# A hybrid decoder layer on one core: x is loaded a second time in eight pieces between weight loads, and the pooling states pass through a staging tile

## The chip, the core and the metric

The kernel runs on one core of one Trainium2 chip. The metric is the device time of one execution in microseconds; the median of 3 runs of the kernel before is 1449.35 (1449.04 to 1449.45).

The engines are called as in the profile: PE (matrix multiply), DVE (vector), ACT (scalar), POOL (GpSimd) and SP (it only issues DMAs). SP's DMAs run on one hardware queue, POOL's on a software queue; both are served by the core's 16 DMA engines.

## The reference, cut to what matters

One layer for 256 prompt tokens and 8 sequences of 8 sample tokens (320 columns in all), model width 2048:

```python
h = rms_norm(x, norm_mix_pre)
proj = h @ w_in                     # q, k, v, g for 4 retention heads, u for 4 pooling groups
...
ret_out = silu(g) * group_norm(retention(q, k, v, S0))
xp = concatenate([buf, u], axis=1)              # buf: the last 15 rows of u, the pooling state
pooled = (windowed sums of xp over 2/4/8/16) / count - u
new_buf = xp[:, -15:, :]                        # an output
pool_out = (pooled per group @ w_pool) * pool_scale
mix = concatenate([ret_out, pool_out]) @ w_out
x = x + rms_norm(mix, norm_mix_post)            # x is needed a second time here
hf = rms_norm(x, norm_ffn_pre)
x = x + rms_norm((silu(hf @ w_gate) * (hf @ w_up)) @ w_down, norm_ffn_post)
```

Outputs are x for all tokens, the new retention states, and `new_buf` for prompt and samples.

## The kernel before, in words

Everything is held transposed, channels on the 128 partitions and the 320 tokens along the row. All matrix products run in three passes of split fp32 (`mm3`, L152 to L156): high weights by high x (L154), high weights by low x (L155), low weights by high x (L156).

**Weights.** The list `queue` holds all weight pieces of 512 KB (128 x 2 x 512) in order of use: `in` (10 groups of 8), `wo` (4 groups of 8, the output projection), then `gu` and `dn` of the feed-forward part. `prepare` (L168) does three things for a piece: SP issues its load into one of four `raw` buffers (L177); ACT casts it to `hi` (L146); DVE computes `lo` = raw - hi (L149). A raw buffer is free again when its `lo` is computed. `hi` and `lo` have four buffers each, free when PE has used the piece. A piece is split two pieces ahead of its use, from wo0 on three. An entry of `queue` can carry a function that runs just before its load; the first eight `in` pieces use it to load `x` for the first time (`xt`).

`project` (L194) runs one group: for each of its 8 pieces (here called chunks) 24 matmuls into four PSUM accumulators. Between chunks it runs side work from a list `stages`, spread evenly by `spread` (L184).

**The stretch around the change.** The order of use is: four heads (qk and vg each), then u1 and u0 (the inputs of pooling groups 3, 2 and 1, 0), then wo0 to wo3. The stages of one group run inside the next: those of the last head inside u1, those of pooling groups 3 and 2 (`pool_group(1, ...)`) inside u0, those of groups 1 and 0 inside wo0. wo0 uses the heads' chunks first and then those of groups 3, 2, 1, 0.

A pooling group has a tile `ue` (in a buffer that a retention state `s_raw` held before), with 15 zero columns, the 256 prompt columns and 8 segments of 15 state columns and 8 new ones. `pool_group` fills it: POOL loads the states (L526), DVE writes u (L527, L528). The stage `windows` stores the new states (L538, L540), loads the group's `w_pool` (`wp`, L542), and adds the windows on DVE (`uw`). `means` gives `pl`, split into `pc` (ACT cast, DVE rest; helper L332, L333), and splits `wp` into `wph` and `wpl`. `mapped` multiplies them on PE (`pp`) and splits the result into `mi_h` and `mi_l` (L336, L337), which wo0's later chunks read.

**The second x.** Behind wo0's code, `x_t` takes over the buffer of `xw_l`, which PE reads until u0 ends, and SP loads all of x into it with one DMA (L616). It is read behind wo3, when the norm of `mix` is there.

Within each engine the order of instructions is set by a scheduler of the framework, from the order and the dependences of the code; each engine then works through its list strictly in order.

Of the kernel before, what the change touches and what calls it, by code (L numbers as in the profile page):

```python
# [18 lines left out]
F32 = mybir.dt.float32  # L19
F32R = mybir.dt.float32r  # L20
# [4 lines left out]
P = 128  # L25
D = 2048
KT = D // P
T = 320
TP = 256
TS = 64  # L30
NB = 8
NS = 8
# [5 lines left out]
PB = 15  # L38
# [60 lines left out]
def layer_kernel(ctx, tc, x, vec, trig, con, mask, pool_in, s_ret, w_in, w_pool, w_out, w_gu, w_dn,  # L99
                 y, o_rp, o_pp, o_rs, o_ps, decay):  # L100
    nc = tc.nc
# [32 lines left out]
    def keep_warm(n, name):  # L134

        ps = aux(f"warm_{name}")
        for i in range(n):
            nc.tensor.matmul(ps[:, :P], ones, ones, start=True, stop=True)
# [20 lines left out]
    queue, raws, parts = [], {}, {}  # L159
    at = dict(load=0, split=0, use=0, ahead=AHEAD[0])  # L160
# [6 lines left out]
    def prepare(between=None):  # L167
        while at["split"] < min(at["use"] + at["ahead"], len(queue)):  # L168
            while at["load"] < min(at["split"] + RAW, len(queue)):
                n = at["load"]  # L170
                src, name, before, _ = queue[n]
                raws[n] = wp.tile([P, 2, 512], F32, tag="raw", name=f"raw_{name}", bufs=RAW)
                step = 1 if n == 0 else 2
                for k in range(0, 2, step):
                    if before:
                        before(k, step)
                    nc.sync.dma_start(out=raws[n][:, k : k + step], in_=src[:, k : k + step])  # L177
                at["load"] += 1
            n = at["split"]
            if queue[n][3]:  # L180
                queue[n][3]()
            parts[n] = halves(raws.pop(n), queue[n][1], 1 if n == 0 else 2, between)
            at["split"] += 1
# [10 lines left out]
    def project(xh, xl, kts, name, stages=(), feed=None, late=0):  # L194

        accs = [psm.tile([P, 512], F32, tag="acc", name=f"acc_{name}_{b}") for b in range(4)]
        n = len(kts) // 2
        steps = spread(stages, n)
        for c in range(n):
            hi, lo = next_weights(feed and (lambda: feed(c)))  # L200
            pairs = [(b, k) for b in range(4) for k in range(2)]
            if c < late:
                pairs.sort(key=lambda bk: bk[1])
            for b, k in pairs:
                bs = slice(b * P, b * P + P)
                kt = kts[2 * c + k]
                mm3(accs[b][:, :T], (hi[:, k, bs], lo[:, k, bs]), (xh[:, kt, :], xl[:, kt, :]),
                    start=c == 0 and k == 0, stop=c == n - 1 and k == 1)
            next(steps)
        return [a[:, :T] for a in accs]  # L210
# [9 lines left out]
    def add_eps(out, acc, sq, width):  # L220

        nc.vector.scalar_tensor_tensor(out, acc, EPS * width / P, sq, op0=ALU.add, op1=ALU.add)

    def slot(i, dtype, name, n=KT):
        return slots.tile([P, n, T], dtype, tag=f"s{i}", name=name)

    xw_h = slot(0, F32R, "xw_h")
    xw_l = slot(1, F32R, "xw_l")
# [4 lines left out]
    order = list(range(2 * H)) + [14, 15, 12, 13, 10, 11, 8, 9]  # L233

    with ExitStack() as ret_ctx:
# [43 lines left out]
        for g in [*range(2 * H), 2 * H + 1, 2 * H]:  # L279
            for c in range(8):  # L280
                queue.append((w_in[g, c], f"in{g}_{c}", (lambda k, step, c=c: x_load(c, k, step)) if g == 0 else None,
                              (lambda c=c: x_split(c)) if g == 0 else None))
        queue += [(w_out[og, order[2 * c] // 2], f"wo{og}_{c}", None, None) for og in range(4) for c in range(8)]
        g0 = 0
        for ph, ng in enumerate(PHASES):
            queue += [(w_gu[g, c], f"gu{g}_{c}", None, None) for g in range(g0, g0 + ng) for c in hf_order]
# [1 line left out]
            g0 += ng  # L288

        r_x = rp.tile([P, T], F32, name="r_x")  # L290
        cs = rp.tile([P, T], F32, name="cs")
        sn = rp.tile([P, T], F32, name="sn")

# [223 lines left out]
        def pool_group(gp, accs):  # L517

            stages = []
            for g_ in (1, 0):  # L520
                g = 2 * gp + g_
                ue = ext(s_raw(f"ue{g}").rearrange("p a e -> p (a e)"))
                us = ue[:, :, PB + TP :].rearrange("p e (b s) -> p e b s", s=SEG)
                nc.gpsimd.memset(ue[:, :, :PB], 0.0)
                for e in range(2):
                    nc.gpsimd.dma_start(out=us[:, e, :, :PB], in_=pool_in[:, 2 * g + e])  # L526
                    nc.vector.tensor_tensor(ue[:, e, PB : PB + TP], accs[2 * g_ + e][:, :TP], r_x[:, :TP], op=ALU.mult)  # L527
                    nc.vector.tensor_tensor(us[:, e, :, PB:], accs[2 * g_ + e][:, TP:].rearrange("p (j b) -> p b j", b=NB),  # L528
                                            r_x[:, TP:].rearrange("p (j b) -> p b j", b=NB), op=ALU.mult)
                stages += pool_stages(g, ue, us)  # L530
            return stages

        def pool_stages(g, ue, us):
            w = WINDOWS[g]
            st = {}

            def windows():
                nc.gpsimd.dma_start(out=o_pp[:, 2 * g : 2 * g + 2], in_=ue[:, :, TP : PB + TP])  # L538
                for e in range(2):
                    nc.gpsimd.dma_start(out=o_ps[:, 2 * g + e], in_=us[:, e, :, NS:])  # L540
                raw = rp.tile([P, 2, TP], F32, tag="st", name=f"wp{g}").rearrange("p a e -> p (a e)")
                nc.gpsimd.dma_start(out=raw, in_=w_pool[g])  # L542
                cur, step, lo_ = ue, 1, 0
                while step < w:
                    shape, tag = ([P, 2, 2, T], "cat_k") if step in (1, 4) else ([P, 2, 2, DK], "kv")
                    flat = rp.tile(shape, F32R, tag=tag, name=f"uw{g}_{step}").bitcast(F32)
                    nx = ext(flat.rearrange("p a s e -> p (a s e)"))
                    lo_ += step
                    nc.vector.tensor_tensor(nx[:, :, lo_:], cur[:, :, lo_:], cur[:, :, lo_ - step : EXT - step], op=ALU.add)
                    cur, step = nx, 2 * step  # L550
                st.update(cur=cur, raw=raw)

            def means():
                cur = st["cur"]
                pl = t640(f"pl{g}")
                nc.vector.scalar_tensor_tensor(pl[:, :, :TP], cur[:, :, PB : PB + TP], 1.0 / w, ue[:, :, PB : PB + TP],
                                               op0=ALU.mult, op1=ALU.subtract)
                for e in range(2):
                    fix = rp.tile([P, PB], F32, tag="fix", name=f"fix{g}_{e}", bufs=2)
                    nc.vector.tensor_tensor(fix, cur[:, e, PB : 2 * PB], cst("rcnt", PB * g, PB), op=ALU.mult)  # L560
                    nc.vector.tensor_tensor(pl[:, e, :PB], fix, ue[:, e, PB : 2 * PB], op=ALU.subtract)
                    nc.vector.scalar_tensor_tensor(
                        pl[:, e, TP:].rearrange("p (j b) -> p b j", b=NB),
                        cur[:, e, PB + TP :].rearrange("p (b s) -> p b s", s=SEG)[:, :, PB:], 1.0 / w,
                        us[:, e, :, PB:], op0=ALU.mult, op1=ALU.subtract)
                pc = rp.tile([P, 2, 2, T], F32R, tag="cat_q", name=f"pc{g}")
                split2(pc[:, 0], pc[:, 1], pl)
                wh = rp.tile([P, 2, TP], F32R, tag="sd_h", name=f"wph{g}").rearrange("p a e -> p (a e)")
                wl = rp.tile([P, 2, TP], F32R, tag="sd_l", name=f"wpl{g}").rearrange("p a e -> p (a e)")
                split2(wh, wl, st["raw"])  # L570
                st.update(pc=pc, wh=wh, wl=wl)

            def mapped():
                pc, wh, wl = st["pc"], st["wh"], st["wl"]
                for e in range(2):
                    ps = aux(f"pp{g}_{e}")
                    for t in range(2):
                        ws = slice(t * DK + e * P, t * DK + e * P + P)
                        mm3(ps[:, :T], (wh[:, ws], wl[:, ws]), (pc[:, 0, t], pc[:, 1, t]), start=t == 0, stop=t == 1)
                    kt = 2 * H + 2 * g + e  # L580
                    split2_scaled(mi_h[:, kt], mi_l[:, kt], ps[:, :T], col("pool_s", 2 * g + e))

            return [windows, means, mapped]
# [4 lines left out]
        def tables():  # L588
            nc.gpsimd.dma_start(out=con_t, in_=con)

        keep_warm(8, "first")
        stages = [idle, idle, tables, lambda: s_load(0), lambda: s_load(1), x_norm]
        for h in range(H):
# [6 lines left out]
                accs = kept  # L600
            stages = head(h, accs, lambda st: project(xw_h, xw_l, range(KT), f"vg{h}", st))
        for gp in (1, 0):
            accs = project(xw_h, xw_l, range(KT), f"u{gp}", stages)
            stages = pool_group(gp, accs)
        at["ahead"] = AHEAD[1]
        accs = project(mi_h, mi_l, order, "wo0", stages + [idle])
# [5 lines left out]
        return fp.tile([P, T], F32, tag="t320", name=name, bufs=6)  # L612

    mix = slot(0, F32, "mix")
    x_t = slot(1, F32, "x_t")
    nc.sync.dma_start(out=x_t, in_=x)  # L616

    def add_square(acc, src, i, name):

# [216 lines left out]
```

## Time and profile before

| | us |
|---|---|
| median of 3 runs | 1449.35 |
| the profiled execution | 1456.14 |
| its span, first to last instruction | 1454.3 |
| PE busy | 1416.4 |
| DVE busy | 755.3 |
| ACT busy | 574.3 |
| POOL busy | 102.3 |

Mean granted clock of PE over the span: 0.988 of full speed. The DMA engines move 233.83 MB, 161 GB/s on average. Busy shares are averages over stages with different limits; where time is lost must be read from the windows and from what each engine waits for.

### The profile page before, as it was taken

To read this page: it belongs to the slowest core of one execution; us is meant where nothing else is said; L and a number is where in the kernel's file an instruction comes from. 1 tells how busy PE (TensorE), PEld (TensorE's weight loads), DVE (VectorE), ACT (ScalarE), POOL (GpSimd) and SP (SyncE) were. 2 spreads that over 40 slices of the span, in tenths; PEclk is the share of its full clock that TensorE was granted. 3 is DMA by queue.
4 is the path that set the end of the run, shared out by engine and by line. 5 is a ranking of instruction groups with operands and counts; after the bars stand their busy time and mean duration, and the time that the engine had idled before them with its cause. 6 is when DMAs were issued, how large, how long until landed. Compare 5 with 4: busy or idle time off the path is not lost.

```text
span 1454.3 us, 22899 instructions
## 1 busy us (share of the span) xinstructions
PE 1416.4 (97%) x9576; PEld 1396.8 (96%) x9576; DVE 755.3 (52%) x981; ACT 574.3 (39%) x732; POOL 102.3 (7%) x153
## 2 busy tenths in 40 slices
PE   8999999999799889999999999999999999999995
PEld 8999999999799889999999999999999999999995
DVE  7657575767443694454334444444454534444455
ACT  6445454543244453333333333223333323333352
POOL 1020202042000340000000000000000000000000
PEclk9999999999899999999999999999999999999998
DMA  9484848488744345445444444444444444444442
GB/s 322 141 258 145 263 142 260 144 233 137 189 146 152 99 131 167 147 145 157 148 148 154 148 145 148 156 147 154 150 145 156 149 146 155 149 145 147 158 131 73
DMA packets 66824, 233.83 MB, mean 161 GB/s; under 512 B 8224, under 2 KB 10208, under 8 KB 66592
## 3 DMA queue, kind: packets, MB, share of 16 engines
q1 hardware_dynamic: 56304, 204.20, 45.4%
q0 software_dynamic: 10416, 28.17, 6.6%
q8 instruction: 75, 1.23, 0.4%
q14 instruction: 29, 0.24, 0.0%
HBM read 216.28 MB, written 16.05 MB: 160 GB/s over the span
## 4 chain that ended last, share of the span: by engine, by line
PE 89%; DMA 3%; DVE 3%; issue 2%; ACT 1%; POOL 1%; SPq 0%; DVEq 0%; ACTq 0%; POOLq 0%
PE acc_gu L156 14%; PE acc_gu L155 14%; PE acc_gu L154 14%; PE acc_dn L156 7%; PE acc_dn L155 7%; PE acc_dn L154 7%; PE acc_qk L154 3%; PE acc_qk L155 3%; PE acc_qk L156 3%; PE acc_vg L155 3%; PE acc_vg L154 3%; PE acc_vg L156 3%; PE acc_wo L156 2%; PE acc_wo L155 2%; PE acc_wo L154 2%
## 5 line engine op out<-in xcount | busy, mean ns | idle before, releaser
L155 PE MATMUL acc_gu<-hf_l,hi_gu 128*128 128x320 f32 x1408 | 437.5, 311 | 5.2 <-DVE hf_l L673 5.1
L154 PE MATMUL acc_gu<-hf_h,hi_gu 128*128 128x320 f32 x1408 | 436.9, 311 | 0.9 <-ACT hf_h L700 0.9
L156 PE MATMUL acc_gu<-hf_h,lo_gu 128*128 128x320 f32 x1408 | 433.8, 310 | 1.6 <-DVE lo_gu L149 1.6
L149 DVE TENSOR_TENSOR lo_gu<-raw_gu,hi_gu 128x1024 fp32r<-128x1024 f32 x176 | 217.9, 1238 | 272.6 <-ACT hi_gu L146 272.6
L146 ACT CAST hi_gu<-raw_gu 128x1024 fp32r<-128x1024 f32 x176 | 184.6, 1049 | 347.6 <-PE acc_gu L155 315.8
L155 PEld LDWEIGHTS acc_gu<-hf_l,hi_gu 128*128 128x128 f32 x1408 | 265.8, 189 | 7.2 <-DVE hf_l L673 7.1
L154 PEld LDWEIGHTS acc_gu<-hf_h,hi_gu 128*128 128x128 f32 x1408 | 265.8, 189 | 1.5 <-ACT hf_h L700 1.1
L156 PEld LDWEIGHTS acc_gu<-hf_h,lo_gu 128*128 128x128 f32 x1408 | 265.1, 189 | 1.9 <-DVE lo_gu L149 1.9
L154 PE MATMUL acc_dn<-a_h,hi_dn 128*128 128x320 f32 x704 | 217.3, 309 | 0.0
L155 PE MATMUL acc_dn<-a_l,hi_dn 128*128 128x320 f32 x704 | 217.3, 309 | 0.0
L156 PE MATMUL acc_dn<-a_h,lo_dn 128*128 128x320 f32 x704 | 215.4, 309 | 0.0
L149 DVE TENSOR_TENSOR lo_dn<-raw_dn,hi_dn 128x1024 fp32r<-128x1024 f32 x88 | 107.7, 1224 | 137.8 <-ACT hi_dn L146 137.7
L146 ACT CAST hi_dn<-raw_dn 128x1024 fp32r<-128x1024 f32 x88 | 92.2, 1048 | 183.0 <-PE acc_dn L155 153.3
L155 PEld LDWEIGHTS acc_dn<-a_l,hi_dn 128*128 128x128 f32 x704 | 132.1, 188 | 0.0
L154 PEld LDWEIGHTS acc_dn<-a_h,hi_dn 128*128 128x128 f32 x704 | 132.1, 188 | 0.0
L156 PEld LDWEIGHTS acc_dn<-a_h,lo_dn 128*128 128x128 f32 x704 | 131.6, 188 | 0.0
L149 DVE TENSOR_TENSOR lo_in<-raw_in,hi_in 128x1024 fp32r<-128x1024 f32 (+1 forms) x81 | 97.8, 1207 | 45.6 <-ACT hi_in L146 41.8
L146 ACT CAST hi_in<-raw_in 128x1024 fp32r<-128x1024 f32 (+1 forms) x81 | 83.5, 1035 | 95.9 <-PE acc_qk L155 45.3
L154 PE MATMUL acc_qk<-xw_h,hi_in 128*128 128x320 f32 x256 | 80.3, 320 | 2.3 <-ACT hi_in L146 2.3
L155 PE MATMUL acc_qk<-xw_l,hi_in 128*128 128x320 f32 x256 | 79.9, 315 | 0.7 <-DVE xw_l L268 0.7
L155 PE MATMUL acc_vg<-xw_l,hi_in 128*128 128x320 f32 x256 | 79.8, 312 | 0.0
L155 PE MATMUL acc_wo<-mi_l,hi_wo 128*128 128x320 f32 x256 | 79.2, 310 | 0.0
(242 smaller groups left out, 1936.0 us busy)
## 6 DMA issues: line engine op xcount, KB each, us to landing
raw_gu<-in_w_gu SPq DMA_DIRECT2D x176, 512.0 KB, 3.6
raw_dn<-in_w_dn SPq DMA_DIRECT2D x88, 512.0 KB, 3.5
raw_in<-in_w_in SPq DMA_DIRECT2D x79, 512.0 KB, 4.4
raw_wo<-in_w_out SPq DMA_DIRECT2D x32, 512.0 KB, 3.6
s_raw<-in_s_ret POOLq DMA_DIRECT2D x16, 512.0 KB, 5.9
out_rs<-s_raw POOLq DMA_DIRECT2D x16, 512.0 KB, 5.6
x_t<-in_x SPq DMA_DIRECT2D x1, 2560.0 KB, 21.9
xt<-in_x SPq DMA_DIRECT2D x7, 320.0 KB, 7.4
```

The source lines that it names most:

```text
L146: nc.scalar.copy(hi[:, ks], src[:, ks])
L149: nc.vector.tensor_tensor(lo[:, ks], src[:, ks], hi[:, ks].bitcast(F32), op=ALU.subtract)
L154: nc.tensor.matmul(ps, wh, xh, start=start, stop=False)
L155: nc.tensor.matmul(ps, wh, xl, start=False, stop=False)
L156: nc.tensor.matmul(ps, wl, xh, start=False, stop=stop)
```

## The change

Two parts, made together.

1. The single load of `x_t` (2560 KB) becomes eight loads of 320 KB. Each is issued by the function of a `wo` entry, so just ahead of the loads of pieces 4 to 7 of wo1 and 0 to 3 of wo2 (`i = 8 * og + c - 12` from 0 to 7); `tc.issue_after` keeps each behind the weight load issued last.
2. The pooling states no longer move straight between memory and the strided columns of `ue`. For each group a tile `p_state[g]` of 240 columns is loaded as whole rows, in one DMA; ACT copies it into `ue` in two pieces. For the new states ACT copies from `ue` back into the same tile, which is stored as whole rows, and the prompt's 30 columns go through `p_prompt`. The tiles lie in buffers that the last head used (`msk` and `q_s`), one of each, so the loads for groups 1 and 0 wait for the stores of groups 3 and 2. The loads are a new stage at the end of each u group's list, which lengthens the list and so moves the other stages a little.

```diff
-                    nc.sync.dma_start(out=raws[n][:, k : k + step], in_=src[:, k : k + step])
+                    at["last"] = nc.sync.dma_start(out=raws[n][:, k : k + step], in_=src[:, k : k + step])
...
-        queue += [(w_out[og, order[2 * c] // 2], f"wo{og}_{c}", None, None) for og in range(4) for c in range(8)]
+
+        def x_again(i):
+
+            if i == 0:
+                late["x_t"] = slot(1, F32, "x_t")
+            with tc.issue_after(at["last"].ins):
+                nc.sync.dma_start(out=late["x_t"][:, 2 * i : 2 * i + 2], in_=x[:, 2 * i : 2 * i + 2])
+
+        for og in range(4):
+            for c in range(8):
+                i = 8 * og + c - 12
+                queue.append((w_out[og, order[2 * c] // 2], f"wo{og}_{c}",
+                              (lambda k, step, i=i: x_again(i)) if 0 <= i < KT // 2 else None, None))
...
+        p_prompt = rp.tile([P, 8, PB], F32, name="p_prompt")
...
-                    nc.gpsimd.dma_start(out=us[:, e, :, :PB], in_=pool_in[:, 2 * g + e])
+                    nc.scalar.copy(us[:, e, :, :PB], p_state[g][:, e])
...
-                nc.gpsimd.dma_start(out=o_pp[:, 2 * g : 2 * g + 2], in_=ue[:, :, TP : PB + TP])
+                gs = slice(2 * g, 2 * g + 2)
+                nc.scalar.copy(p_prompt[:, gs], ue[:, :, TP : PB + TP])
                 for e in range(2):
-                    nc.gpsimd.dma_start(out=o_ps[:, 2 * g + e], in_=us[:, e, :, NS:])
+                    nc.scalar.copy(p_state[g][:, e], us[:, e, :, NS:])
+                nc.gpsimd.dma_start(out=o_pp[:, gs], in_=p_prompt[:, gs])
+                nc.gpsimd.dma_start(out=o_ps[:, gs], in_=p_state[g])
...
+        p_state = {}
+
+        def pool_states(gp):
+
+            flat = [rp.tile([P, 384], F32, tag="msk", name=f"ps{2 * gp + 1}"),
+                    rp.tile([P, 2, NB, 2, NS], F32R, tag="q_s", name=f"ps{2 * gp}").bitcast(F32)
+                    .rearrange("p t b s j -> p (t b s j)")]
+            for g_, f in zip((1, 0), flat):
+                g = 2 * gp + g_
+                p_state[g] = f[:, : 2 * NB * PB].rearrange("p (e b s) -> p e b s", e=2, b=NB)
+                nc.gpsimd.dma_start(out=p_state[g], in_=pool_in[:, 2 * g : 2 * g + 2])
+
...
-            accs = project(xw_h, xw_l, range(KT), f"u{gp}", stages)
+            accs = project(xw_h, xw_l, range(KT), f"u{gp}", stages + [lambda: pool_states(gp)])
...
-    x_t = slot(1, F32, "x_t")
-    nc.sync.dma_start(out=x_t, in_=x)
+    x_t = late["x_t"]
```

SP's queue, the loads of wo0's pieces 4 to 7 and wo1's first ones. Before:

```order
L177 DMA raw_wo_4_3810<-in_w_out 128x1024
L177 DMA raw_wo_5_3860<-in_w_out 128x1024
L177 DMA raw_wo_6_3866<-in_w_out 128x1024
L616 DMA x_t<-in_x 128x5120
L177 DMA raw_wo_7_3905<-in_w_out 128x1024
L177 DMA raw_wo_0_3952<-in_w_out 128x1024
L177 DMA raw_wo_1_4000<-in_w_out 128x1024
```

Now, from wo1's piece 0 on (the number behind `raw_wo_` is the piece):

```order
L177 DMA raw_wo_0_3967<-in_w_out 128x1024
L177 DMA raw_wo_1_4015<-in_w_out 128x1024
L177 DMA raw_wo_2_4054<-in_w_out 128x1024
L177 DMA raw_wo_3_4101<-in_w_out 128x1024
L291 DMA x_t<-in_x 128x640
L177 DMA raw_wo_4_4149<-in_w_out 128x1024
L291 DMA x_t<-in_x 128x640
L177 DMA raw_wo_5_4181<-in_w_out 128x1024
```

The large load stood ahead of wo0's piece 7. Now nothing stands there; the first piece of it stands ahead of wo1's piece 4, and from there on weight loads and pieces alternate until wo2's piece 3.

ACT's list in u0, from the cast of piece 4 to the first `pc`. Before:

```order
L146 CAST hi_in_4_3598<-raw_in_4_3456 128x1024
L332 CAST mi_h<-o_t_3128 128x640
L146 CAST hi_in_5_3646<-raw_in_5_3506 128x1024
L146 CAST hi_in_6_3687<-raw_in_6_3549 128x1024
L146 CAST hi_in_7_3734<-raw_in_7_3596 128x1024
L332 CAST pc_3589<-pl_3579 128x640
```

Now (`ps` is a staging tile; 3820 and 3819 are those of groups 0 and 1, 3457 that of group 3):

```order
L556 COPY ps_3457<-ue_3491 128x120
L146 CAST hi_in_4_3605<-raw_in_4_3461 128x1024
L146 CAST hi_in_5_3653<-raw_in_5_3511 128x1024
L541 COPY ue_3861<-ps_3820 128x8x15 x2
L541 COPY ue_3853<-ps_3819 128x8x15 x2
L347 CAST mi_h<-o_t_3129 128x640
L146 CAST hi_in_6_3696<-raw_in_6_3556 128x1024
L146 CAST hi_in_7_3743<-raw_in_7_3603 128x1024
L347 CAST pc_3596<-pl_3586 128x640
```

Four copies of the loaded states now stand ahead of the cast of u0's piece 6.

POOL's list in u0 and wo0 now (before, 16 DMAs of 128x8x15 and four of 128x2x15 stood between the same `out_rs` and `wp` loads):

```order
L557 DMA out_pp<-p_prompt 128x30
L558 DMA out_ps<-ps_3458 128x240
L557 DMA out_pp<-p_prompt 128x30
L558 DMA out_ps<-ps_3457 128x240
L619 DMA ps_3820<-in_pool_in 128x240
L619 DMA ps_3819<-in_pool_in 128x240
L560 DMA wp_3914<-in_w_pool 128x512
```

The states of groups 0 and 1 are loaded behind the stores of groups 2 and 3, and ahead of `w_pool`'s load for group 1.

## Rows read from the trace of the kernel before

**Rows 1.** The page, part 1: busy time, share of the span, instructions.
```profile
PE 1416.4 (97%) x9576; PEld 1396.8 (96%) x9576; DVE 755.3 (52%) x981; ACT 574.3 (39%) x732; POOL 102.3 (7%) x153
```
**Rows 2.** Windows of 10 us: length, PE, PEld, DVE, ACT, POOL busy, PEclk, DMA, GB/s.
```profile
380.00:390.00 10.00, 2.17 (x12) 1.55 (x10) 2.80 (x5) 3.88 (x7) 0.00 (x0) 0.72 0.81 183
390.00:400.00 10.00, 9.27 (x51) 9.27 (x52) 5.16 (x6) 3.81 (x7) 0.00 (x0) 0.76 0.42 150
```
**Rows 3.** Timeline of PE in wo0: start, length, instruction, [idle before, releaser].
```profile
381.22 0.31 PE L156 MATMUL acc_wo<-mi_h,lo_wo 128*128 128x320 f32 x1
389.19 0.64 PE L154 MATMUL pp<-pc,wph 128*128 128x320 f32 x1 [7.66 <-ACT pc L332]
390.73 0.64 PE L155 MATMUL pp<-pc,wph 128*128 128x320 f32 x1 [0.90 <-DVE pc L333]
...
394.83 0.31 PE L155 MATMUL acc_wo<-mi_l,hi_wo 128*128 128x320 f32 x1
```
**Rows 4.** Timeline of ACT in the same stretch.
```profile
386.12 1.04 ACT L146 CAST hi_wo<-raw_wo 128x1024 fp32r<-128x1024 f32 x1 [15.38 <-DMA raw_wo<-in_w_out]
...
387.49 0.61 ACT L332 CAST wph<-wp 128x512 fp32r<-128x512 f32 x1
...
388.42 0.72 ACT L332 CAST pc<-pl 128x640 fp32r<-128x640 f32 x1
```
**Rows 5.** DMA issues at 358.5, 363.5, 361.7 and 354.9 us: count, KB, us to landing.
```profile
x_t<-in_x SPq DMA_DIRECT2D x1, 2560.0 KB, 21.9
...
raw_wo<-in_w_out SPq DMA_DIRECT2D x1, 512.0 KB, 22.5
...
wp<-in_w_pool POOLq DMA_DIRECT2D x1, 256.0 KB, 21.6
...
wp<-in_w_pool POOLq DMA_DIRECT2D x1, 256.0 KB, 5.0
```
**Rows 6.** DMA issues of weights: the one at 333.1 us, and the twelve from 400 to 440.
```profile
raw_wo<-in_w_out SPq DMA_DIRECT2D x1, 512.0 KB, 15.7
...
raw_wo<-in_w_out SPq DMA_DIRECT2D x12, 512.0 KB, 3.5
```
**Rows 7.** Landing of the pooling states: out_ps (8 stores), in_pool_in (8 loads).
```profile
DMA to landing us min/median/max: 7.4/14.4/21.9
...
DMA to landing us min/median/max: 3.6/5.0/13.4
```
**Rows 8.** Timeline of PE at the end of u0.
```profile
353.71 0.81 PE L154 MATMUL pp<-pc,wph 128*128 128x320 f32 x2 [0.27 <-ACT pc L332]
...
355.89 0.42 PE L155 MATMUL pp<-pc,wph 128*128 128x320 f32 x1 [0.20 <-DVE pc L333]
```
**Rows 9.** Timelines of ACT and DVE in wo1: one piece, and the fourth after it.
```profile
408.37 1.05 ACT L146 CAST hi_wo<-raw_wo 128x1024 fp32r<-128x1024 f32 x1 [1.74 <-PE acc_wo L155]
...
409.45 1.23 DVE L149 TENSOR_TENSOR lo_wo<-raw_wo,hi_wo 128x1024 fp32r<-128x1024 f32 x1 [1.56 <-ACT hi_wo L146]
...
422.45 1.05 ACT L146 CAST hi_wo<-raw_wo 128x1024 fp32r<-128x1024 f32 x1 [2.47 <-PE acc_wo L155]
```
**Rows 10.** Page, part 6: first load of x; its issues; GB/s, 300 to 312 us, 40 slices.
```profile
xt<-in_x SPq DMA_DIRECT2D x7, 320.0 KB, 7.4
...
L258 SPq DMA_DIRECT2D xt<-in_x x9: 327/379/932, 0.7 to 20.9; - x9
...
GB/s 102 72 7 0 0 0 0 0 0 68 164 287 328 178 178 232 259 246 273 314 314 260 191 205 218 294 321 225 184 259 348 417 423 437 410 410 423 410 423 410
```
**Rows 11.** Timelines of DVE, ACT, PE in u1 and u0; DMA issues of 40 to 120 us.
```profile
326.45 0.26 DVE L528 TENSOR_TENSOR ue<-acc_u,r_x 128x64 f32<-128x64 f32 x1
...
318.71 0.27 ACT L479 COPY o_t<-os 128x128 f32<-128x128 f32 x1 [1.14 <-PE os L478]
...
346.97 0.31 PE L154 MATMUL acc_u<-xw_h,hi_in 128*128 128x320 f32 x1
...
x_d<-cr_sb POOLq DMA_DIRECT2D x4, 32.0 KB, 2.5
```

More of the change, by code (lines that the diff above doesn't have):

```diff
@@ L222, in add_eps @@
         nc.vector.scalar_tensor_tensor(out, acc, EPS * width / P, sq, op0=ALU.add, op1=ALU.add)
+    late = {}
     def slot(i, dtype, name, n=KT):
```

## The prediction

> **What bounds the kernel now.** I read the page first. TensorE (PE) is busy 97% of the span [rows 1], so only a stretch where PE stands still, or runs at a lower clock, can give time back. The windows of 10 us find one large stretch: between 380 and 390 us PE is busy 2.17 of 10 us, and the granted clock is 0.72 there and 0.76 in the next 10 us [rows 2], against 1.00 in the windows around. The reader should see that this is in the first group of the output projection (wo0), where the pooling groups are finished.
>
> PE's timeline shows the hole itself [rows 3]. The matmul at 381.22 is followed by one at 389.19, after a wait of 7.66 us for ScalarE's (ACT's) cast of `pc`; a second wait of 0.90 us for VectorE's (DVE's) half of `pc` follows, and the normal pace is back at 394.83. The matmul at 389.19 takes 0.64 us: PE comes out of the idle time at the lower of its two clock levels (1.2 and 2.4 GHz).
>
> ACT's timeline says why `pc` came late [rows 4]. ACT works in order. A cast `hi_wo` stood at its head until 386.12, 15.38 us of it waiting for a weight piece from memory; `wph` and `pc`, which need nothing of that piece, ran behind it at 387.49 and 388.42. The DMA view gives the last step [rows 5]: the 2560 KB load of `x_t` was issued at 358.5 and took 21.9 us; the weight load behind it on the same queue (issued 363.48) took 22.5, and `w_pool`'s last load, on the other queue (issued 361.65), 21.6. An undisturbed weight load takes 3.5 [rows 6].
>
> There is an earlier disturbance too: a weight load issued at 333 took 15.7 us [rows 6], while the pooling states moved as 128x8 runs of 15 floats. The stores of those states land after 7.4 to 21.9 us though each is only 60 KB, the loads after 3.6 to 13.4 [rows 7]. PE lost only 0.27 and 0.20 us there [rows 8].
>
> **The change, part by part.**
>
> *The one large load leaves the queue.* The place of `x_t`'s load, ahead of wo0's last weight piece, becomes empty, as the excerpt of SP's queue shows. The missed piece should land in about 3.5 instead of 22.5 us, so about 367, before its ACT cast can use a buffer: that is when PE leaves the fourth chunk, two chunks of 3.52 us before 381.36, so 374.3. What is late next is the last `pc`. From the cast's start at 386.12 to `pc`'s end at 388.42 + 0.72 are 3.0 us, and 1.6 later, at 390.73, PE had the DVE half too [rows 3, 4]; counted from 374.3 that is 378.9, against 381.36 when PE wants it. The slack is 2.4 us, so I cost the rest of the hole at nothing. Gain: 16 matmuls start from 389.19 up to 394.83. At the normal pace of 0.1467 us (four chunks of 24 matmuls in the 14.08 us between the casts at 408.37 and 422.45 [rows 9]) the one at 394.83 would have started at 381.36 + 16 x 0.1467 = 383.71. That is **11.1 us**: 7.8 of idle time, 0.9 of the second wait, and 2.4 of low clock.
>
> *Eight pieces of 320 KB go behind later weight loads.* They stand ahead of the loads of wo1_4 to wo2_3, as the same excerpt shows. One chunk of weights is used in 3.52 us. A weight load is issued when the DVE half four chunks before frees its buffer (409.45 + 1.23 = 410.68) and is wanted at 422.45 [rows 9]: 11.8 us, of which 3.5 are used, so 8.3 are spare. A piece of 320 KB costs between nothing and 7.4 us, what such pieces took at the kernel's start among other loads [rows 10]. Even at 7.4 a weight load would land after 10.9 of 11.8 us. The queue must move 832 KB in 3.52 us, 236 GB/s; it has sustained 410 and more [rows 10]. I cost the pieces at 0. `x_t` itself is first read only behind wo3, a whole group after the last piece.
>
> Against the split stands a rule of the Trainium skill: "DMA: Bandwidth & Descriptors", Anatomy of one DMA, fits a software-queue DMA as some 2.0 us fixed plus bytes over 436 GB/s; carried over to this queue as an estimate, eight pieces pay 14 us more than one load. By that, if the fixed parts came one after another, 16 + 6 - 8.3 = 13.7 us would be uncovered and the gain gone. The trace doesn't bear this out: at the start nine such loads were issued between 0.7 and 20.9 us, each with a weight load beside it, and took 7.4 us apiece [rows 10]; one after another, nine would have needed 67 us, so such loads overlap.
>
> *The states move as whole rows.* Eight loads and eight stores of 60 KB in short runs become four loads and four stores of 120 KB in rows of 960 bytes. POOL loses eight issues. What this frees on the 16 DMA engines lets wo0's first two pieces land before ACT wants them, so the two small waits go: **0.47 us** [rows 8]. In exchange ACT gets 20 copies (two in, two out and one of the prompt for each of four groups). The nearest row is a 128x128 copy, 0.27 us [rows 11], so 5.4 us together. ACT is busy 3.9 of 10 us around the hole and mostly waits for PE's buffers, so this hides; the price without that cover would be 5.4.
>
> *What the scheduler moved.* One more stage in the list brings `cr_3`'s matmuls forward by about 16 matmuls, with `hi_s_3` ahead of `hi_in_4`. Between nothing and one cast plus its DVE half (1.05 + 1.23 = 2.3 us) could appear as a new wait. I take 0.4, near the small waits of [rows 8], because casts run two chunks ahead.
>
> Sum: -11.1 - 0.5 + 0.4 = **-11.2 us**. Against the profiled execution's own 1456.14 that is 1444.9; the median of the runs, 1449.35, lies 6.8 below it, and I take the difference over: **1438.2 us**. How much of those 6.8 sits in the hole can't be seen. If all of it did, the gain would be 4.4.
>
> **The rivals.**
>
> *A rest of the hole stays.* `w_pool`'s last load took 21.6 us though it isn't in `x_t`'s queue. If it still landed at 383.2, `wph`, `mi_h` and `pc` would follow (0.6 + 0.5 + 0.7), PE would wait 3.7 + 0.9 us and again lose some 2.4 at the low clock: 7.0 of the 11.2 stay, 1445.1 us. Against it: the same load for the group before, issued at 354.94 before `x_t`, took 5.0 [rows 5].
>
> *The states' round trip blocks ACT (slower).* The third fence shows the place: the copies of the second pair's states now stand in ACT's queue ahead of `hi_in_6`, and they need the first pair's stores to land (the staging tiles are reused) and then the new loads. The first pair's last value is written at 326.71 [rows 11]; behind `hi_in_3` and two copies, 1.6 us, the last store goes out near 329 with its issue. PE wants `hi_in_6` at 346.97 [rows 11]; four copies (1.1), `mi_h` (0.7, as `pc` of the same shape [rows 4]) and the cast (1.05 [rows 9]) come before, so both trips may take 15.1 us. The nearest quiet rows give 2.5 us for 32 KB [rows 11] and 5.0 for 256 KB [rows 5], so 5.0 to 10.0 for both trips. At the medians of the short-run transfers, 14.4 + 5.0 [rows 7], PE waits 4.3 us plus 2.4 of low clock, and 1444.9 is left. At their maxima, 21.9 + 13.4, it waits 20.2 + 2.4, 11.4 more than is gained: 1460.8 us. It decides from a round trip of 23.9 us on. For it: two DMAs in a row on a critical queue; against: the short runs that made these times are gone.
>
> *The pieces hold up the weights.* To cancel the gain they would have to hold the queue by 11.2 + 8.3 = 19.5 us together, nearly as long as the whole load took (21.9). At that, 13.6 us are uncovered: 1451.8. At 19.5 the time is unchanged, 1449.4. For it: one queue serves both; against: 8.3 us of spare time for each load. By the Trainium skill's rule above the pieces would take 22 us, and the time would be 1451.9.
>
> **How the numbers follow.** Forecast 0.70, rest of the hole 0.15, round trip 0.08 (half of it slower than before), pieces 0.05 (two thirds unchanged or slower), and 0.02 that nothing changes because the hole only moves. A measurement of this kernel can tell about 0.2%, 2.9 us, from no change. So faster 0.70 + 0.15 + 0.01 = 0.86, within 0.2% 0.07, slower 0.07. The forecast alone reaches from 1436.0 (without the 0.4, and a hole 1.8 longer in the runs, twice the 0.9 by which two late landings differ [rows 5]) to some 1442. The range goes on to 1445.2, which takes in the rest of the hole, a hole smaller by the profile's 6.8, and a round trip at the old medians.
>
> **What would show it.** Right: in the changed profile PE's wait for `pc` L154 is gone, the window that holds wo0's end has PE near 10 of 10 and a clock of 1.00; raw_wo lands in about 4 us all through wo0, with the pieces some 5; the stores of the states land in under 6. Wrong: a wait of PE in the u0 stage ahead of its seventh chunk, released by `hi_in`, with ACT held by a copy that waits for DMA; ACT casts in wo1 or wo2 that wait for raw_wo; or `pc` still over 381 us with `wph` waiting for `wp`.

## The result, and the profile after

| | before | changed |
|---|---|---|
| median of 5 runs each, us | 1449.35 (1448.98 to 1449.85) | 1442.76 (1441.49 to 1444.18) |
| ratio | | 0.995, 95% interval 0.9939 to 0.9961 |
| the profiled execution, us | 1456.14 | 1442.52 |
| its span | 1454.3 | 1440.8 |

The kernel is faster by 6.6 us, some 0.45%; forecast were 11.2. Between the two profiled executions the difference is 13.6 us. Both numbers matter below.

The windows of wo0 after the change (start and end in us), with the columns of [rows 2]:

```profile
360.00:370.00 10.00, 10.00 (x70) 10.00 (x69) 8.88 (x21) 3.89 (x4) 0.00 (x0) 1.00 0.51 164
370.00:380.00 10.00, 10.00 (x71) 10.00 (x70) 4.70 (x6) 5.13 (x7) 0.00 (x0) 1.00 0.52 166
380.00:390.00 10.00, 10.00 (x71) 10.00 (x70) 5.12 (x7) 6.34 (x13) 0.00 (x0) 1.00 0.60 212
390.00:400.00 10.00, 10.00 (x70) 10.00 (x70) 3.70 (x5) 3.14 (x3) 0.00 (x0) 1.00 0.71 237
```

PE is busy throughout, and the clock is full in every window. The place of the hole, in PE's and ACT's timelines after (compare [rows 3] and [rows 4]):

```profile
370.70 1.05 ACT L146 CAST hi_wo<-raw_wo 128x1024 fp32r<-128x1024 f32 x1 [2.76 <-PE acc_wo L155]
...
372.71 0.62 ACT L347 CAST wph<-wp 128x512 fp32r<-128x512 f32 x1
...
373.66 0.72 ACT L347 CAST pc<-pl 128x640 fp32r<-128x640 f32 x1
```

```profile
379.12 0.31 PE L154 MATMUL pp<-pc,wph 128*128 128x320 f32 x1
```

ACT's cast now waits for PE, not for memory, and the cast of `pc` ends 4.7 us before PE wants it (373.66 + 0.72 against 379.12). The matmul that resumed at 389.19 starts at 379.12, at the normal pace. The DMA issues after, 318 to 400 us (count, KB, median us to landing):

```profile
raw_wo<-in_w_out SPq DMA_DIRECT2D x18, 512.0 KB, 3.6
x_t<-in_x SPq DMA_DIRECT2D x7, 320.0 KB, 4.1
...
wp<-in_w_pool POOLq DMA_DIRECT2D x2, 256.0 KB, 3.3
out_ps<-ps POOLq DMA_DIRECT2D x4, 120.0 KB, 2.5
ps<-in_pool_in POOLq DMA_DIRECT2D x2, 120.0 KB, 3.3
...
```

The medians are 2.5 to 4.1 us, where the late loads and the stores of [rows 5 to 7] took 14 to 22. Between 20 and 450 us the trace lists no wait of PE at all after the change. The longest over the whole span are:

```profile
PE acc_gu L155 <- DVE hf_l L702: 5.8, 6, 2.4
PE acc_gu L156 <- DVE lo_gu L149: 1.6, 1, 1.6
PE acc_qk L154 <- DVE xw_h L269: 1.2, 1, 1.2
...
```

No wait of the pooling stretch is left. Those of `acc_gu` lie where the feed-forward part begins (450 to 520 us), that of `acc_qk` in the first 20 us.

### The profile page after: what moved, and what is told of

Read it like the earlier page. It is cut to its first block, busy times and chain, and to the rows that moved or that the text cites. A ratio compares the mean times of both kernels' runs of the same rounds, so it can differ in the third digit from the quotient of the medians.

```text
span 1440.8 us, 22920 instructions
## 1 busy us (share of the span) xinstructions
PE 1412.0 (98%) x9576; PEld 1393.3 (97%) x9576; DVE 755.8 (52%) x981; ACT 578.8 (40%) x752; POOL 91.9 (6%) x145
## 2 busy tenths in 40 slices
DMA packets 67704, 233.83 MB, mean 162 GB/s; under 512 B 8208, under 2 KB 10192, under 8 KB 67600
## 4 chain that ended last, share of the span: by engine, by line
PE 95%; DVE 3%; ACT 1%; DMA 1%; issue 0%; SPq 0%; DVEq 0%; ACTq 0%
PE acc_gu L156 14%; PE acc_gu L154 14%; PE acc_gu L155 14%; PE acc_dn L154 7%; PE acc_dn L156 7%; PE acc_dn L155 7%; PE acc_qk L154 3%; PE acc_vg L155 3%; PE acc_qk L155 3%; PE acc_vg L154 3%; PE acc_wo L156 3%; PE acc_vg L156 3%; PE acc_wo L155 3%; PE acc_wo L154 3%; PE acc_qk L156 3%; PE acc_u L154 1%
```

## The experiments

The result alone doesn't say which half of the change did it, nor why the profiles differ by 13.6 us and the medians by 6.6. Eleven runs were made, on three chips; each ratio is against the kernel before on the same chip, where that kernel's median was 1455.73 (E1 to E4), 1454.53 (E5 to E8) and 1454.48 (E9 to E11): close to the execution that was profiled first, and above the 1449.35 of the runs in the table.

### E1: the kernel before again

No edit.

> The kernel before, once more, unchanged. The profile read for the prediction was of an execution 6.8 us longer than the median. Theory 1: those 6.8 us lay in the hole of wo0, so in an ordinary execution near 1449.4 us the waits of PE for pc are together 3 to 5 us instead of 8.6, and the loss with the low clock is 5 to 7 us instead of 11.1. Rival: the hole is as long as before (8.6 us of waits), and the 6.8 us lay elsewhere; then the change gave back some 4.5 us somewhere else. Ratio to the kernel before 1.000.

Measured: 1454.94 us, ratio 0.9999 (0.9989 to 1.0009). Its profiled execution took 1454.89 us. PE's waits in it:

```profile
PE pp L154 <- ACT pc L332: 8.2, 1, 8.2
...
PE pp L155 <- DVE pc L333: 1.1, 2, 0.9
```

Neither case of the expectation came up as it was put, since no execution near 1449.4 us was to be had. At 1455 us the hole is as long as in the profile read for the prediction. So that profile wasn't odd; the 1449.35 of the first set is the number that stands apart.

### E2: only the second load of x

(against the kernel before; `x_again` is that of the change)

```diff
-        queue += [(w_out[og, order[2 * c] // 2], f"wo{og}_{c}", None, None) for og in range(4) for c in range(8)]
+        for og in range(4):
+            for c in range(8):
+                i = 8 * og + c - 12
+                queue.append((w_out[og, order[2 * c] // 2], f"wo{og}_{c}",
+                              (lambda k, step, i=i: x_again(i)) if 0 <= i < KT // 2 else None, None))
...
-    nc.sync.dma_start(out=x_t, in_=x)
```

> Only the second load of x is changed (eight pieces from wo1_4 on); the pooling states move as before, in short runs. Theory A, the single load is the cause by itself: the hole is gone, 1443 us (-6 to -7), raw_wo for wo0's last piece lands in under 8 us. Theory B, the load is slow only because the short runs hold the DMA engines, so that either part alone is enough: also about 1443. Theory C, the short runs are the cause by themselves: wo0's last pieces and w_pool's last load still land after 12 us or more, and no more than a third of the gain is there, 1447 us or more.

Measured: 1447.46 us, ratio 0.9937 (0.9921 to 0.9953): some two thirds of what the other part gives alone (E3). None of the three cases came up whole: the last pieces land late, as theory C says (16.9 us, the median of the two issued from 362.4 us on, and 17.6 for `w_pool`'s last load), but far more than a third of the gain is there. Three views, the windows, ACT's timeline, and the DMA issues of 350 to 372 us, in which no load of x is in flight:

```profile
360.00:370.00 10.00, 10.00 (x70) 10.00 (x69) 9.97 (x23) 4.51 (x5) 2.86 (x4) 1.00 0.98 79
370.00:380.00 10.00, 10.00 (x71) 10.00 (x70) 2.09 (x5) 0.27 (x1) 0.00 (x0) 1.00 1.00 131
380.00:390.00 10.00, 7.02 (x35) 6.52 (x35) 6.76 (x9) 5.97 (x9) 0.00 (x0) 0.83 0.81 258
```

```profile
380.38 1.05 ACT L146 CAST hi_wo<-raw_wo 128x1024 fp32r<-128x1024 f32 x1 [10.11 <-DMA raw_wo<-in_w_out]
```

```profile
raw_wo<-in_w_out SPq DMA_DIRECT2D x6, 512.0 KB, 11.8
wp<-in_w_pool POOLq DMA_DIRECT2D x2, 256.0 KB, 10.7
out_ps<-ue POOLq DMA_DIRECT2D x4, 60.0 KB, 13.5
...
```

This is the reading that says most. With the large load gone, the DMA engines are still busy 98 to 100% of the time, and move 79 and 131 GB/s. The same windows of the changed kernel show 51 and 52% at 164 and 166. Split by queue (packets, MB, share of the 16 engines' time; q0 is POOL's, q1 is SP's with the weights), the windows 360 to 370 and 370 to 380 us of E2 give

```profile
q0 software_dynamic: 173, 0.36, 57.1%
q1 hardware_dynamic: 121, 0.43, 40.5%
...
q1 hardware_dynamic: 318, 1.18, 90.9%
q0 software_dynamic: 72, 0.12, 7.6%
```

and q1 in the changed kernel

```profile
q1 hardware_dynamic: 432, 1.57, 49.2%
...
q1 hardware_dynamic: 501, 1.66, 51.7%
```

So it isn't only that the stores take engine time for themselves: the packets of the weights occupy the engines some 3 and 2.5 times as long per byte while the stores are under way. A high busy share here is slow transfers, not many bytes. A smaller hole remains: PE waits 1.9 + 1.1 us there.

### E3 and E6: only the states as whole rows

```diff
-    x_t = late["x_t"]
+    x_t = slot(1, F32, "x_t")
+    nc.sync.dma_start(out=x_t, in_=x)
```

(against the changed kernel; the `queue` of wo is that of the kernel before)

> Only the pooling states are changed (whole rows through the staging tile); x_t is loaded by one DMA of 2560 KB ahead of wo0's piece 7, as before. Theory A, the single load is the cause by itself: the load still takes some 20 us, the hole stays, 1448 to 1449.5 us. Theory B: at some 400 GB/s the load takes 6 to 8 us, piece 7 lands by about 370, the hole is gone, 1443 us. Theory C: also 1443 us.

Measured: 1442.30 us, ratio 0.9907 (0.9891 to 0.9924): the whole gain. DMA issues of 350 to 372 us, and the window:

```profile
raw_wo<-in_w_out SPq DMA_DIRECT2D x5, 512.0 KB, 4.8
x_t<-in_x SPq DMA_DIRECT2D x1, 2560.0 KB, 10.3
...
out_ps<-ps POOLq DMA_DIRECT2D x2, 120.0 KB, 7.1
...
```

```profile
360.00:370.00 10.00, 10.00 (x70) 10.00 (x69) 8.50 (x20) 3.58 (x4) 0.00 (x0) 1.00 0.93 358
```

The weight load just behind `x_t`, issued at 358.62:

```profile
raw_wo<-in_w_out SPq DMA_DIRECT2D x1, 512.0 KB, 9.0
```

The same load of 2560 KB, at the same place in the queue, takes 10.3 instead of 21.9 us, at 358 GB/s in the window, and the weight load behind it 9.0 instead of 22.5. That piece has landed by 367.6, and no cast of ACT waits for memory. Theory A falls. Run beside the changed kernel:

> Only the states moved as whole rows, once more, beside the changed kernel. Theory 2, the eight pieces of x add nothing once the short runs are gone: within 1 us of the changed kernel. Rival: the 2 us of spare time for w_pool's last load are too few with one large load, PE waits for pc in some executions, 1 to 3 us longer than the changed kernel.

Measured: median 1445.01 us, ratio 0.9925 (0.9911 to 0.9939), beside 1441.99 and 0.9920 (0.9906 to 0.9934) for the changed kernel (E5). The medians are 3.0 us apart where the expectation allowed 1, so by them it was missed. The runs lie near 1442 or near 1445 us (1441.72, 1442.06; 1445.01, 1445.19, 1445.45), which seemed to speak for the rival. But single runs near 1445 are there in E4, E5, E7 and E10 too, and the long one that was traced (E5, below) lost its time at the kernel's start. The profiled execution here, in which PE waits for `pc` not at all, is one of the short ones; none of the long three was traced. The eight pieces add nothing that these runs can tell.

### E4: one load of x, later

```diff
             if i == 0:
                 late["x_t"] = slot(1, F32, "x_t")
-            with tc.issue_after(at["last"].ins):
-                nc.sync.dma_start(out=late["x_t"][:, 2 * i : 2 * i + 2], in_=x[:, 2 * i : 2 * i + 2])
+                with tc.issue_after(at["last"].ins):
+                    nc.sync.dma_start(out=late["x_t"], in_=x)
```

> As the changed kernel, but the second load of x is one DMA of 2560 KB, at the place of the first piece (ahead of wo1_4). It tells the place from the split. If the place alone matters: the weight load behind it lands after 8 to 12 us, inside the 11.8 us that a weight load has, PE waits for nothing in wo1, ratio to the changed kernel 1.000, 1442.8 us. If the split matters: the weights behind the load come 2 to 10 us late, PE waits in wo1, 1445 to 1455 us.

Measured: 1441.99 us, ratio 0.9910 (0.9894 to 0.9925). The load lands in 9.4 us and PE waits for nothing in wo1. The split isn't needed either.

### E5: the changed kernel on another chip

No edit.

> The changed kernel once more, unchanged, beside the kernel before on one chip and beside the part kernels. Theory 1, the hole of the kernel before is of different length from chip to chip, and the changed kernel has none: 1441.5 to 1443.5 us wherever it runs, however long the kernel before takes here (1449 to 1456). Rival: both shift together by the same share from chip to chip, and the ratio stays near 0.995.

Measured: 1441.99 us, ratio 0.9920 (0.9906 to 0.9934), outside the first interval of 0.9939 to 0.9961. The changed kernel takes the time that it took in the first set (1442.76), the kernel before 5.2 us more than there (1454.53). Theory 1 holds in that form: the kernel before differs from one set of runs to another, the changed one doesn't. That it is the hole that differs isn't shown.

Its profiled execution was the longest of the five, 1445.75 us, and shows where 3 us between executions lie. The first 20 us of it, and of the changed kernel's first profile (1442.52 us):

```profile
0.00:20.00 20.00, 15.26 (x71) 14.47 (x72) 10.84 (x19) 11.74 (x19) 3.01 (x10) 0.83 0.88 315
```

```profile
0.00:20.00 20.00, 16.88 (x91) 15.86 (x92) 11.78 (x21) 12.69 (x20) 3.01 (x10) 0.91 0.90 331
```

By 20 us it has 71 matmuls behind it instead of 91, and its second group (vg of the first head) begins at 41.2 instead of 38.3 us. The difference is the start: the weight load of 512 KB issued at 5.5 us, for one, lands after 11.0 us instead of 9.8. Since both are executions of one kernel, it has nothing to do with the change.

### E7 and E8: only the stores, only the loads

E7 stages the stores and loads the states in short runs; E8 stages the loads and stores in short runs. Against E3:

```diff
-                    nc.scalar.copy(us[:, e, :, :PB], p_state[g][:, e])
+                    nc.gpsimd.dma_start(out=us[:, e, :, :PB], in_=pool_in[:, 2 * g + e])
...
-                nc.gpsimd.dma_start(out=p_state[g], in_=pool_in[:, 2 * g : 2 * g + 2])
```

```diff
-                    nc.scalar.copy(p_state[g][:, e], us[:, e, :, NS:])
-                nc.gpsimd.dma_start(out=o_ps[:, gs], in_=p_state[g])
+                    nc.gpsimd.dma_start(out=o_ps[:, 2 * g + e], in_=us[:, e, :, NS:])
```

(E8 also stores `o_pp` straight from `ue`.)

> As states_only, but the states are loaded in short runs straight into the columns of ue, as before; only the stores are staged as whole rows. x_t by one load at its old place. Theory 3, the short stores hold the DMA engines (they landed after 14 to 15 us, the short loads after 5): the hole stays away, within 1.5 us of states_only, 1441.5 to 1444. Rival, loads and stores matter alike: x_t lands after 15 us or so and half of the hole is back, 1446 or more.

> As states_only, but the new states are stored in short runs straight from ue, as before; only the loads are staged as whole rows. x_t by one load at its old place. Theory 3: the hole is back as in the kernel before, x_t lands after 18 us or more, within 2 us of the kernel before on this chip. Rival, loads and stores matter alike: about half way between.

Measured: E7 1442.38 us, ratio 0.9922 (0.9908 to 0.9935); E8 1454.60 us, ratio 1.0007 (0.9995 to 1.0018). The two could not be further apart. DMA issues of 348 to 372 us, first E7, then E8:

```profile
raw_wo<-in_w_out SPq DMA_DIRECT2D x6, 512.0 KB, 4.5
x_t<-in_x SPq DMA_DIRECT2D x1, 2560.0 KB, 10.3
...
```

```profile
raw_wo<-in_w_out SPq DMA_DIRECT2D x7, 512.0 KB, 18.6
x_t<-in_x SPq DMA_DIRECT2D x1, 2560.0 KB, 21.0
...
out_ps<-ue POOLq DMA_DIRECT2D x4, 60.0 KB, 17.2
...
```

With short stores the load of x takes 21.0 us, with short loads 10.3. The short loads run at another time, from 309.7 us on; the weights issued beside them (309 to 323 us) land after 5.1 us in E7, where with whole-row loads they took 3.5 (E3) and 5.2 (E8). wo's weights issued behind the first stores (323 to 345 us) take 12.4 us in E8 and 3.5 in E7. PE's wait for `pc` is back in E8, at full length:

```profile
PE pp L154 <- ACT pc L334: 9.2, 2, 7.6
```

### E9: no stores of the samples' states at all

```diff
-                for e in range(2):
-                    nc.gpsimd.dma_start(out=o_ps[:, 2 * g + e], in_=us[:, e, :, NS:])
```

(against the kernel before)

> The kernel before without the eight stores of the samples' new pooling states (this output is left out); nothing is staged, ACT has no copy, the states are loaded in short runs, x_t by one load at its old place. Theory 3, the short stores are the whole cause and the staging costs nothing: 1441.5 to 1444 us, as the changed kernel. Rival, ACT's copies cost something that the gain hides: 1 to 5 us below the changed kernel, 1437 to 1441. If a hole stays without the stores, theory 3 falls: 1446 or more.

Measured: 1441.78 us, ratio 0.9912 (0.9895 to 0.9928). Eight stores of 60 KB, 0.49 of the 233.83 MB that the kernel moves, make the whole difference. The four stores of the prompt's rows, 15 KB each and in 60-byte runs as well, are still there, so they aren't the cause. Without any staging the time is that of the changed kernel, so ACT's copies cost nothing that shows. (This kernel leaves out an output; it serves the comparison alone.)

### E10: rows of 480 bytes

```diff
-                nc.gpsimd.dma_start(out=o_ps[:, gs], in_=p_state[g])
+                for e in range(2):
+                    nc.gpsimd.dma_start(out=o_ps[:, 2 * g + e], in_=p_state[g][:, e])
```

(against E7)

> As stores_only, but each group's states are stored by two DMAs with rows of 480 bytes instead of one with 960. If the harm comes from the number of short writes (8192 of 60 bytes before, 1024 here, 512 in stores_only): within 1.5 us of stores_only, landing in under 9 us. If any row under 512 bytes is slow by itself: landing and x_t's load get longer by some us, and a part of the hole may be back, 1444 to 1449.

Measured: 1442.33 us, ratio 0.9921 (0.9906 to 0.9935), as E7. The landing of its eight stores, and then that of the eight in E8:

```profile
DMA to landing us min/median/max: 1.8/3.5/8.8
```

```profile
DMA to landing us min/median/max: 7.3/15.6/23.6
```

The DMAs carry the same 60 KB each; the runs differ, 480 bytes against 60, and with them their number, 1024 against 8192. The runs here don't tell length from number.

### E11: the kernel before a third time

No edit.

> The kernel before once more, for a look at its hole on whatever chip this is. Theory 1: an execution near 1449.4 us has PE waits for pc of 2 to 5 us together, one near 1454 to 1456 us has 8 to 10.

Measured: one execution, 1454.66 us, with waits for `pc` of 8.0 + 1.1 us, as expected for that time. An execution near 1449 us has not been seen in a trace.

No version without the short stores beats another by more than these runs can tell: their lowest times lie between 1441.23 (E9) and 1442.08 (E7). Of those that write every output E7 needs the fewest changes.

## Why the prediction was right, and where not

**The hole and its chain: right.** PE's waits for `pc`, the low clock behind them and the small waits of [rows 8] are gone; no new wait took their place. The terms of the hole add up in the profiles. Counted to the sixteenth matmul behind the first `pp`, 394.83 before and 379.12 + 16 x 0.1467 = 381.47 after, 13.4 us are gained. Of these 11.1 are the hole as costed, 0.5 the small waits, 0.3 a wait at 304 us that wasn't in the sum. Of the last 1.5, 0.9 lie in the first 40 us (vg of the first head begins at 39.2 and 38.3), which differ by as much from execution to execution; some 0.6 lie in u1 and u0 and weren't traced to a wait. The 0.4 set aside for what the scheduler moved didn't come: no such wait is in the trace.

**The step that failed: "The one large load leaves the queue", for 11.1 us.** The load was a victim like the weights behind it. Left where it was, beside states in whole rows (E3), it costs nothing; moved alone (E2), it brings two thirds. The likely reason, argued from E2's rows and not tested by itself: with the load gone there is less to push through the slowed engines, and the cast that waits for the last weights starts at 380.38 instead of 386.12. "The states move as whole rows" was priced at 0.47 us, and is by itself worth the whole gain (E3), all of it from the stores (E7, E8, E9). The two parts don't add: either shortens the same hole, and the second finds little or nothing left.

The evidence lay in [rows 7], stores of 60 KB that land after 14.4 us while loads of the same shape take 5.0. I let the states disturb the weights around 333 us, and didn't ask when the second four stores go out. POOL's timeline before shows them around the issue of `x_t` at 358.5, and the window behind it has the engines' share near 1 at 203 GB/s, where they had moved 410 and more [rows 10]:

```profile
356.66 0.90 POOL L540 DMA_DIRECT2D out_ps<-ue  x1 [1.15 <-DVE ue L528]
...
358.83 1.79 POOL L540 DMA_DIRECT2D out_ps<-ue  x2
...
362.90 0.92 POOL L540 DMA_DIRECT2D out_ps<-ue  x1
```

```profile
360.00:370.00 10.00, 10.00 (x70) 10.00 (x69) 9.32 (x17) 5.03 (x7) 2.80 (x4) 1.00 1.01 203
```

No rival of the prediction names these stores as the cause of the hole. That the hole went whole all the same was luck: the cause sat in the part made for 0.47 us.

The Trainium skill bears on this: "DMA: Bandwidth & Descriptors", Specifications, says that transfers under 512 bytes make the engine read, modify and write. For the stores in 60-byte runs the traces agree in direction (15.6 us against 3.5). For the loads in 60-byte runs (4.3 us median in E7, against 3.0 for whole rows of twice the bytes in E3) and for the stores in rows of 480 bytes (3.5 us) the traces show no loss of time, so nothing here shows a line at 512 bytes. Whether a read-modify-write is the mechanism no run shows; how the stores slow the packets of other queues stays open.

**The rule about fixed costs did not carry over.** The Trainium skill states it in "DMA: Bandwidth & Descriptors", Anatomy of one DMA, for a software queue; here the pieces go through SP's hardware queue. With the pieces among them the weight loads of 380 to 412 us land in 3.5 us and the pieces in 4.1; nothing is uncovered. The price 0 was right. Two readings behind it were off, without weight: of the nine first loads of x [rows 10] seven have 320 KB and two 160 (7.4 and 3.3 us), so one after another they would need some 58 us and not 67; and 832 KB of 1024 bytes in 3.52 us are 242 GB/s and not 236.

**The rivals.** The rest of the hole: no; `w_pool`'s loads land after 3.3 us. The states' round trip: the last store of the first pair is issued at 326.70, ACT's copies run at 332.60, without a wait for the loads:

```profile
326.70 0.54 POOL L558 DMA_DIRECT2D out_ps<-ps  x1
...
328.94 0.54 POOL L619 DMA_DIRECT2D ps<-in_pool_in  x1 [0.46 <-DMA out_ps<-ps]
```

```profile
332.60 0.87 ACT L541 COPY ue<-ps 128x120 f32<-128x120 f32 x4
```

That is at most 5.9 us of the 15.1 allowed, near the lower of the two quiet estimates (5.0 to 10.0). The pieces: no, as above.

**The size: the difference of the profiles was carried over to the median.** Measured is a gain of 6.6 us where 11.2 were forecast: 4.6 above the centre, inside the range. The changed kernel's profiled execution took 1442.52 us (forecast for it: 1444.9), and its median is the same, 1442.76. The 6.8 us by which the kernel before's profile lay above its median are absent after the change: 13.6 - 6.8 = 6.8, and 6.6 was measured. So the case that the prediction set beside its sum, a gain of 4.4 with all of the 6.8 lost, was nearer to the truth than the centre. On the chip of E5 the same change gains 12.5 us, more than forecast; which of the two a set of runs shows, the prediction couldn't know. That the hole was shorter in those first runs fits this arithmetic and E5; it isn't shown, since no execution near 1449 us was traced, and why it should be shorter there stays open.

## What to carry to other kernels

Where loads land late, ask who shares the DMA engines before blaming the largest transfer. Compare the engines' busy share with the GB/s moved, and look at what is issued at the same time on other queues: a small store in short runs is a suspect whatever its bytes. When a change has two parts that touch one hole, price each with the other undone; their gains needn't add. And a difference between two profiled executions can be taken over to medians only as far as the part that is removed has the same length in both.

## What the runs showed of the hardware

Eight stores of 60 KB in runs of 60 bytes, issued from another queue, cost 12.2 us (E8 against E7). While the last four of them were under way, the 16 DMA engines were busy for 98 to 100% of 20 us at 79 and 131 GB/s, with the weights' packets taking some 3 and 2.5 times as long per byte as in the changed kernel (E2); a 2560 KB load took 21.0 instead of 10.3 us (E8 against E7). Loads in the same 60-byte runs cost no time that shows (E7), and stores of the same size in 480-byte rows land in 3.5 us (E10).
